# Low parts of queries and scores on VectorE, an empty step ahead of a head's first values, and one convolution product copied out of PSUM

## The chip, the cores and the metric

The kernel runs on one core of a Trainium2 chip. The metric is the device time of one execution in microseconds (us); a run's time is given as the median of several executions. The engines are named as in the profile: PE (TensorE matmuls), PEld (its weight loads), DVE (VectorE), ACT (ScalarE), POOL (GpSimd) and SP (SyncE, which issues most DMAs).

## What is computed

Two layers of a decoder trunk on 1024 tokens of width 1024. Each layer projects the normed input into eight heads of width 256 (four mLSTM heads, four retention heads), runs each head chunk by chunk, gates and norms the result, and projects it back:

```
h = rmsnorm(x) * (1 + scale) + shift;  p = h @ w_in[l]
q, k = silu(causal_dwconv(mq, mk))            # mLSTM heads; retention heads: q, k = rotary(rq, rk)
s   = einsum('bhld,bhsd->bhls', q, k) * w_intra
num = einsum('bhls,bhsv->bhlv', s, v) + w_inter * einsum('bhvk,bhlk->bhlv', C, q)
C   = decay * C + einsum('bhs,bhsv,bhsk->bhvk', w_end, v, k)
y = gated_norm(num / den);  x = x + gate * (concat(y) @ w_out[l])
```

The output is the final RMSNorm of x.

## The kernel before

**Precision.** Every float32 operand of a large product is split into a high part (a rounded copy, made by ACT) and a low part (the operand less its high part, one subtraction). A product is then three matmuls: high by high, high by low, low by high (`mm3`, L180 to L183). So each operand needs one ACT instruction and one subtraction before PE can start on it. The low parts of weights are made by `low` (L411 to L414, mostly DVE), those of queries and keys by `split_to` (L880 to L882, here always POOL), those of scores at L1084 (POOL).

**The projections.** Work on PE stands in program order. It is a list of *slots*. A slot of a q, k, z or o job is one of seven block products (a11, S1, S2, a12, S3, S4, a22) with 12 matmuls of 128x512; a slot of a value job (v) has 24 matmuls of 128x256. The products gather in PSUM banks, two of tag x and two of tag z (`ps_x`, `ps_z`). `pair_product` (L762) hands each finished piece to a `done` function. For the four mLSTM heads' q and k that is the start of `conv_chain` (L884): one ACT instruction (L889) and three DVE instructions (L894), which read the piece from where it lies. The last piece of a job, `done(1, 0, bank["X"])`, lies in PSUM, so bank X is busy until the third L894 has read it. The order of the jobs in a layer is the string `plan`.

**The attention of a head.** After each slot `tick()` runs what is due. A head's attention is the string `TABLE` (L985): one step per tick, in which `q`, `k`, `v` load a chunk's queries, keys and values, `Q` and `K` split them into high and low parts, `S` makes scores (PE L1045 and L181 to L183, then DVE L1061 to L1064 or L1073 and L1075, then ACT L1083 for the high part sH and L1084 for the low part sL), `U` updates the state, `V` makes values (PE). There are four chunks, 0 to 3. The first values of a head, `V001`, come four steps after `S0` and use no state: PE first runs the products with sH of chunk 0, then those with sL (L1126). When a head's table reaches index `RELEASE`, the next head may begin.

**The order elsewhere.** DVE, ACT, POOL and SP each work through a queue in order. That order is not written by hand: a scheduling layer sets it when the program is built, out of program order and its own estimates. Some instructions are marked to stay in program order (`late`). A small change of the program can therefore move many instructions on these engines.

**Shared buffers.** Twelve buffers of tag acc serve all intermediate 128x512 pieces; queries have two buffers, keys one, sH and sL one each.

## Time and profile before

| | |
|---|---|
| median of 3 runs | 2192.43 us (2189.73 to 2194.45) |
| the profiled execution, its own time | 2190.59 us |
| its span, first to last instruction | 2188.9 us |
| mean granted TensorE clock | 0.989 |
| PE busy | 2105.7 us (96%) |
| DVE busy | 1775.1 us (81%) |
| ACT busy | 1149.3 us (53%) |
| POOL busy | 671.1 us (31%) |

The span is what the instruction records cover; the execution's own time is 1.7 us longer. The table of waits lists, for an engine, who waited for whom: total us, times, longest. Rows of the groups by line give busy us and mean ns of one. Rows of the windows give, for each stretch of the span, the busy us of each engine with the number of instructions that began in it, then the granted clock (PEclk), the share of the DMA engines and GB/s.

### The profile page before, as it was taken

The page shows a single profiled execution, that of the slowest core. Times are in us where ns is not written, and L with a number is a line of the kernel's source. Part 1 is how long each engine was busy: PE and PEld are TensorE (multiplying, and loading weights), DVE is VectorE, ACT ScalarE, POOL GpSimd, SP SyncE. Part 2 cuts the span into 40 slices and gives each one's busy share as a digit, 9 for nine tenths or more (in the row PEclk, how much of TensorE's full clock was granted, in tenths as well). Part 3 has the DMA queues.
Part 4 walks back from the last instruction along what each step waited for, and adds up shares of the span by engine and source line. Part 5 has one row for each costly group of instructions (what it writes and reads, how often), then busy time and mean ns, then how long its engine had stood idle before and what let it go on. Part 6 is the DMA issues. An engine that isn't in the chain of part 4 may idle for free.

```text
span 2188.9 us, 34934 instructions
## 1 busy us (share of the span) xinstructions
PE 2105.7 (96%) x11489; PEld 1818.2 (83%) x11489; DVE 1775.1 (81%) x3287; ACT 1149.3 (53%) x2151; POOL 671.1 (31%) x616
## 2 busy tenths in 40 slices
PE   7899999999999999999999999999999999999998
PEld 5698889887988778888887889788988887888887
DVE  6897897999889898874639688898898888978563
ACT  7545335345565656653545434444556565665343
POOL 1421123233232333324565113322323332231313
PEclk9999999999999999999999999999999999999999
DMA  8268779788787767786633777977876676687874
GB/s 292 60 202 236 219 220 269 205 225 235 195 236 191 188 179 215 195 273 230 209 108 93 188 196 210 252 204 215 230 196 193 187 220 189 185 205 248 228 252 119
DMA packets 451971, 448.43 MB, mean 205 GB/s; under 512 B 191218, under 2 KB 308410, under 8 KB 451788
## 3 DMA queue, kind: packets, MB, share of 16 engines
q1 hardware_dynamic: 432060, 410.27, 61.3%
q0 software_dynamic: 19584, 35.66, 10.7%
q8 instruction: 90, 1.47, 0.3%
q14 instruction: 93, 0.76, 0.1%
q10 hardware_dynamic: 144, 0.26, 0.0%
HBM read 322.76 MB, written 123.31 MB: 204 GB/s over the span
## 4 chain that ended last, share of the span: by engine, by line
PE 47%; DVE 11%; DMA 5%; issue 3%; ACT 1%; POOL 1%; SPq 1%; DVEq 0%; POOLq 0%; ACTq 0%
PE px L181 6%; PE px L182 6%; PE px L183 6%; PE pz L181 5%; PE pz L182 5%; PE pz L183 4%; PE pa L183 4%; PE pa L181 3%; PE pa L182 3%; DVE R L413 2%; DVE acc L894 2%; PE pa L1135 1%; DMA acc<-kfr 1%; PE pa L1045 1%; DVE R L718 1%
## 5 line engine op out<-in xcount | busy, mean ns | idle before, releaser
L408 ACT CAST wH<-R 128x512 fp32r<-128x512 f32 x616 | 378.9, 618 | 494.4 <-PE px L182 161.0
L413 DVE TENSOR_TENSOR R<-R,wH 128x512 fp32r<-128x512 f32 x544 | 404.2, 748 | 123.4 <-ACT wH L408 121.1
L181 PE MATMUL px<-b,wH 128*128 128x512 f32 x912 | 359.9, 395 | 3.5 <-ACT acc L780 2.7
L182 PE MATMUL px<-b,wH 128*128 128x512 f32 x912 | 358.6, 393 | 0.0
L183 PE MATMUL px<-b,R 128*128 128x512 f32 x912 | 358.0, 393 | 0.0
L182 PE MATMUL pz<-b,wH 128*128 128x512 f32 x704 | 275.3, 391 | 1.6 <-DVE b L1271 1.6
L181 PE MATMUL pz<-b,wH 128*128 128x512 f32 x704 | 276.5, 393 | 0.0
L183 PE MATMUL pz<-b,R 128*128 128x512 f32 x704 | 275.0, 391 | 0.0
L714 POOL DMA_DIRECT2D R<-in_w_blk_dram x104 | 92.6, 890 | 379.1 <-DMA R<-in_w_blk_dram 191.1
L181 PEld LDWEIGHTS px<-b,wH 128*128 128x128 f32 x912 | 172.9, 190 | 39.1 <-ACT acc L780 3.9
L183 PEld LDWEIGHTS px<-b,R 128*128 128x128 f32 x912 | 172.9, 190 | 37.3
L182 PEld LDWEIGHTS px<-b,wH 128*128 128x128 f32 x912 | 172.8, 189 | 32.9
L181 PE MATMUL px<-wH,b 128*128 128x256 f32 (+1 forms) x576 | 173.2, 301 | 13.8 <-DVE acc L894 5.0
L182 PE MATMUL px<-R,b 128*128 128x256 f32 (+1 forms) x576 | 172.4, 299 | 8.3 <-DVE R L413 8.3
L183 PE MATMUL px<-wH,b 128*128 128x256 f32 (+1 forms) x576 | 171.9, 298 | 0.0
L183 PEld LDWEIGHTS pz<-b,R 128*128 128x128 f32 x704 | 132.5, 188 | 28.4
L182 PEld LDWEIGHTS pz<-b,wH 128*128 128x128 f32 x704 | 132.8, 189 | 27.5 <-DVE b L1271 2.4
L181 PEld LDWEIGHTS pz<-b,wH 128*128 128x128 f32 x704 | 132.8, 189 | 25.9 <-ACT acc L780 0.4
L882 POOL TENSOR_TENSOR kc<-acc,kc 128x512 fp32r<-128x512 f32 x64 | 91.7, 1434 | 193.3 <-ACT kc L881 169.3
L413 POOL TENSOR_TENSOR R<-R,wH 128x512 fp32r<-128x512 f32 x72 | 96.6, 1344 | 164.8 <-ACT wH L408 145.8
L882 POOL TENSOR_TENSOR q<-acc,q 128x512 fp32r<-128x512 f32 x64 | 93.5, 1461 | 131.8 <-ACT q L881 123.5
L181 PE MATMUL pz<-wH,b 128*128 128x256 f32 (+1 forms) x448 | 133.8, 299 | 0.0
(348 smaller groups left out, 5203.9 us busy)
## 6 DMA issues: line engine op xcount, KB each, us to landing
R<-in_w_blk_dram SPq DMA_DIRECT2D x276, 256.0 KB
vdr<-acc SPq DMA_DIRECT2D x128, 256.0 KB
ring<-vdr SPq DMA_DIRECT2D x64, 512.0 KB
R<-in_w_out_dram SPq DMA_DIRECT2D x128, 256.0 KB
R<-in_w_blk_dram POOLq DMA_DIRECT2D x104, 256.0 KB, 4.7
R<-in_w_val_dram SPq DMA_DIRECT2D x80, 256.0 KB
gdr<-acc SPq DMA_DIRECT2D x64, 256.0 KB
acc<-in_w_ada_dram SPq DMA_DIRECT2D x64, 256.0 KB
```

The lines of the kernel that those rows point to most:

```text
L181: PE.matmul(o, lt[0], rt[0], start=start, stop=False, skip_group_check=more)
L182: PE.matmul(o, lt[0], rt[1], start=False, stop=False, skip_group_check=more)
L183: PE.matmul(o, lt[1], rt[0], start=False, stop=stop, skip_group_check=more)
L408: A.copy(h, r)
L413: eng.tensor_tensor(lo, r, f(h), ALU.subtract)
L714: G.dma_start(raw[n], src, accum_op=ALU.add)
L718: V.tensor_tensor(raw[n], raw[one], raw[two], ALU.add)
L882: eng.tensor_tensor(dst[1], src, f(dst[0]), ALU.subtract)
L894: V.scalar_tensor_tensor(acc[:, e:], pt[:, o + e - d:o + HALF - d], wcol, acc[:, e:], ALU.mult, ALU.add)
L1045: PE.matmul(pd, piece(kx[j], i, dt, tt * P, P), qd, start=dt == 0 and i == 0, stop=dt == 1 and i == 1)
L1135: PE.matmul(pi[:, 0:W], piece(qs[j], i, dt, tt * P, P), state[part][:, dt, 0:W], start=part + dt + i == 0, stop=ml and part + dt == 2)
```

## The change

Four edits, all in the code shown above:

- The low part of a query chunk is subtracted by DVE; that of a key chunk stays on POOL (`split_qk`).
- The low part of the scores is subtracted by DVE (in `scores`).
- `TABLE` has an empty step between `Q1` and `V001 t1`, and one empty step less between `V21` and `V30`; `RELEASE` goes from 22 to 23, so it still names the step of `S3`.
- A q or k job of an mLSTM head that is followed by a value job copies its last product from bank X to an acc buffer by ACT, and its convolution reads the copy. In the two plans that is `k0` in the first layer and `k1` in the second.

```diff
-    def pair_product(F, done, loose=False, conv=False):
+    def pair_product(F, done, loose=False, conv=False, free=False):
...
                     halo("S1", bank["X"])
-                    done(1, 0, bank["X"])
+                    last = bank["X"]
+                    if free:
+                        last = wt("acc", 512, NACC)
+                        A.copy(last, bank["X"])
+                    done(1, 0, last)
...
-    TABLE = ("q0 k0 d0 t0", "", "v0", "Q0 K0 m0 d1", "s0 k1", "S0", "m1 q1 K1", "v1", "Q1", "V001 t1", "S1 k2 q2", "U01",
+    TABLE = ("q0 k0 d0 t0", "", "v0", "Q0 K0 m0 d1", "s0 k1", "S0", "m1 q1 K1", "v1", "Q1", "", "V001 t1", "S1 k2 q2", "U01",
              "s1 d2 K2", "v2 Q2", "V10 U2 m2", "S2", "t2 d3", "V11 U3 k3", "s2 q3", "v3 K3", "Q3 m3", "V20 U4",
-             "S3", "", "V21 U5", "", "", "", "V30", "V31", "")
-    RELEASE = 22
+             "S3", "", "V21 U5", "", "", "V30", "V31", "")
+    RELEASE = 23
...
-                split_to((t[:, 0:512], t[:, 512:1024]), raw)
+                split_to((t[:, 0:512], t[:, 512:1024]), raw, V if what == "q" else G)
...
-            G.tensor_tensor(lo, src, f(hi), ALU.subtract)
+            V.tensor_tensor(lo, src, f(hi), ALU.subtract)
...
-            return pair_product(F, conv_done(l, h, which), conv=True)
+            return pair_product(F, conv_done(l, h, which), conv=True, free=free)
...
-                going[j] = job_product(*jobs[j])
+                going[j] = job_product(*jobs[j], j + 1 < len(jobs) and jobs[j + 1][0] == "v")
```

In the changed kernel, lines behind L794 have numbers higher by 4 (L882 becomes L886, L1084 becomes L1088, L1126 becomes L1130).

**Low parts.** Before, on POOL, in the second mLSTM head of the first layer (kc and q are low parts of keys and queries, sL that of the scores of chunk 0, dm a mask that is read from a DMA's landing):

```order
L882 TENSOR_TENSOR kc_8696<-acc_8618,kc_8696 128x512
L714 DMA R_8737<-in_w_blk_dram 128x512
L882 TENSOR_TENSOR q_8761<-acc_8694,q_8761 128x512
L1034 AFFINE_SELECT dm_8941<-dm_8941 128x128 x2
L1084 TENSOR_TENSOR sL_8727<-acc_8646,sH_8726 128x384
L714 DMA R_8951<-in_w_blk_dram 128x512
L1185 TENSOR_TENSOR rsd_8833<-va_8832,mhalf 128x2
L882 TENSOR_TENSOR kc_8943<-acc_8852,kc_8943 128x512
```

The same two subtractions now, on DVE, among the low parts of weights (R), the convolutions (L898, L903) and a transpose of an earlier chunk (zt):

```order
L903 SCALAR_TENSOR_TENSOR acc_8606<-acc_8716,acc_8606 128x512
L413 TENSOR_TENSOR R_8783<-R_8638,wH_8762 128x512
L898 SCALAR_TENSOR_TENSOR acc_8657<-acc_8561,cols_497,acc_8657 128x512
L886 TENSOR_TENSOR q_8759<-acc_8690,q_8759 128x512
L1088 TENSOR_TENSOR sL_8727<-acc_8625,sH_8726 128x384
L1201 STREAM_TRANSPOSE zt_8755<-nd_8566 128x2x8x32
L413 TENSOR_TENSOR R_8834<-R_8467,wH_8786 128x512
L898 SCALAR_TENSOR_TENSOR acc_8657<-acc_8561,cols_497,acc_8657 128x512
```

What stood on POOL behind a load and a mask stands on DVE behind weights' and convolutions' work; the keys' subtraction is alone on POOL.

**The empty step.** Before, on PE, the end of the fourth slot behind the scores of that head's chunk 0, then its first values (ring holds the value chunk):

```order
L181 MATMUL pz_8768<-b_1256,wH_8663 128x512
L182 MATMUL pz_8768<-b_1257,wH_8663 128x512
L183 MATMUL pz_8768<-b_1256,R_8704 128x512
L1126 MATMUL pa_8786<-ring_353,sH_8726 128x258 x2
L1126 MATMUL pa_8789<-ring_353,sH_8726 128x258 x4
L1126 MATMUL pa_8786<-ring_353,sL_8727 128x258
L1126 MATMUL pa_8789<-ring_353,sL_8727 128x258 x2
```

Now a fifth slot, on the px bank, stands between the pz slot and the values; its end reads:

```order
L181 MATMUL px_8421<-b_1573,wH_8698 128x512
L182 MATMUL px_8421<-b_1574,wH_8698 128x512
L183 MATMUL px_8421<-b_1573,R_8730 128x512
L1130 MATMUL pa_8812<-ring_353,sH_8726 128x258 x2
L1130 MATMUL pa_8815<-ring_353,sH_8726 128x258 x4
L1130 MATMUL pa_8812<-ring_353,sL_8727 128x258
L1130 MATMUL pa_8815<-ring_353,sL_8727 128x258 x2
```

So 60 instead of 48 matmuls stand between scores and first values here. Where two heads overlap, the last two value steps of the earlier head (`V30`, `V31`) lay in that interval too; now only `V31` does, and the count goes from 69 to 72.

**The copy.** Before, on ACT, at the end of job `k1` of the second layer (px_19489 is the bank X of that job, acc_19799 the convolution's sum):

```order
L408 CAST wH_19943<-R_19695 128x512
L1107 CAST cH_19774<-cf_19331 128x516
L897 ACTIVATE acc_19759<-acc_19678 128x512
L889 ACTIVATE acc_19799<-px_19489,cols_1153 128x512
L889 ACTIVATE acc_19810<-acc_19538,cols_1153 128x512
```

Now, at the same place (px_19449 is that bank):

```order
L901 ACTIVATE acc_19739<-acc_19626 128x512
L1194 ACTIVATE nd_19499<-nd_19499,nmu_19741,rsd_19694 128x256
L797 COPY acc_19763<-px_19449 128x512
L1194 ACTIVATE nd_19499<-nd_19499,nmu_19741,rsd_19694 128x256
L408 CAST wH_19915<-R_19664 128x512
L893 ACTIVATE acc_19765<-acc_19763,cols_1153 128x512
L893 ACTIVATE acc_19773<-acc_19491,cols_1153 128x512
```

The copy is the last reader of the bank on ACT, and the convolution's reads (L893 and the three L898 on DVE) name the copy.

More of the change, by code (lines that the diff above doesn't have):

```diff
@@ L1623, in tile_hybrid_trunk, with job_product @@
         launch(adaptive(l, gcol, gb), 40 if l else 30)
-        def job_product(what, arg):
+        def job_product(what, arg, free=False):
             h = arg[0]
```

## The prediction

> **What bounds the kernel now.** I read the page first, then PE's waits, then the granted clock behind the longest of them, then the order of events at three places. The page's engine line, and its line of DVE's busy tenths in 40 slices of the span:

> ```profile
> PE 2105.7 (96%) x11489; PEld 1818.2 (83%) x11489; DVE 1775.1 (81%) x3287; ACT 1149.3 (53%) x2151; POOL 671.1 (31%) x616
> ...
> DVE  6897897999889898874639688898898888978563
> ```

> PE is busy 2105.7 of 2188.9 us and none of its matmuls go away, so the change can only act on the other 83 us and on PE's clock. DVE has a 9 (90% or more) in 11 of 40 slices and an 8 in 17 more: it is the next to become the bound. PE's waits, those that the edits touch and the largest that they don't:

> ```profile
> PE px L182 <- DVE R L413: 8.3, 3, 5.6
> ...
> PE pa L1126 <- ACT sH L1083: 8.2, 4, 4.1
> PE pa L1126 <- POOL sL L1084: 6.3, 7, 2.9
> ...
> PE px L181 <- DVE acc L894: 5.0, 1, 5.0
> ...
> PE pa L183 <- POOL kc L882: 3.1, 3, 1.3
> ```

> First values (L1126) cost 8.2 + 6.3 = 14.5 us, bank X behind a convolution 5.0, low parts of keys 3.1. A long stall costs a second time. Windows of 4 us at three first values and behind the convolution stall:

> ```profile
> 544.00:548.00 4.00, 2.65 (x11) 2.27 (x12) 4.00 (x6) 1.43 (x4) 2.64 (x3) 0.67 0.85 226
> 548.00:552.00 4.00, 4.00 (x10) 3.04 (x10) 1.58 (x7) 1.09 (x2) 1.48 (x3) 0.50 0.97 315
> 726.00:730.00 4.00, 4.00 (x13) 3.15 (x12) 1.18 (x9) 0.40 (x2) 1.00 (x2) 0.57 0.84 189
> 1408.00:1412.00 4.00, 3.12 (x10) 2.59 (x10) 4.00 (x10) 1.64 (x4) 2.25 (x3) 0.62 0.85 280
> 1720.00:1724.00 4.00, 3.89 (x22) 3.89 (x23) 4.00 (x11) 2.33 (x5) 2.74 (x3) 0.63 0.05 15
> ```

> PEclk is the figure after the busy times. At 0.50 a window does half its work, so the loss is 4 us times (1 - PEclk): 1.3 + 2.0 at 544, 1.7 at 726, 1.5 at 1408, which is 6.5 us behind first values, and 1.5 us behind the convolution.

> **First values: empty step and scores' low part.** At the head whose instruction order is shown above, PE and POOL:

> ```profile
> 709.36 0.40 PE L181 MATMUL pz<-b,wH 128*128 128x512 f32 x1
> ...
> 721.10 1.00 PE L1126 MATMUL pa<-ring,sH 128*128 128x258 f32 x6 [0.69 <-ACT sH L1083]
> 724.99 0.63 PE L1126 MATMUL pa<-ring,sL 128*128 128x258 f32 x3 [2.89 <-POOL sL L1084]
> ```

> ```profile
> 722.06 1.91 POOL L1034 TENSOR_SCALAR_AFFINE_SELECT dm<-dm 128x128 f32<-128x128 f32 x2 [3.51 <-DMA dm<-mdr]
> 723.95 0.98 POOL L1084 TENSOR_TENSOR sL<-acc,sH 128x384 fp32r<-128x384 f32 x1
> ```

> The 48 matmuls of four slots run from 709.36 to 720.41 (721.10 less the wait), so one takes 11.05 / 48 = 0.23 us and a slot 2.8 us. POOL was idle, but a mask that waits for its DMA stood ahead of sL. Here the fifth slot covers sH (0.69 late), and DVE can make sL without the mask: both waits go. In the heads where `V30` leaves the interval, the cover grows from 69 to 72 matmuls: twelve long ones in, nine short ones out. Six of the short kind begin within 1.00 us above, at most 0.17 apart, and half a long one's 0.23 is the least, so the gain is 12 x 0.23 less 9 x 0.12 to 0.17: 1.2 to 1.7 us, say 1.6. Of that kind is the longest stall:

> ```profile
> 543.61 0.28 DVE L1064 TENSOR_TENSOR acc<-acc 128x128 f32<-128x128 f32 x1
> ```

> ```profile
> 544.74 0.51 PE L1126 MATMUL pa<-ring,sH 128*128 128x256 f32 x2 [4.08 <-ACT sH L1083]
> ```

> What came last is the DVE queue: the scores' last DVE instruction ended at 543.9, sH a little later. If DVE comes no earlier, 4.08 - 1.6 = 2.5 us stays; the new order does put the scores' rows a little nearer to the front. Of 14.5 + 6.5 = 21 us I leave 3: **-18 us** (from -21, all gone, to -9, if the stalls that DVE ends stay with their clock).

> [...] The row at 726 shows 0.57 behind stalls of 0.69 and 2.89 us, so I keep the rows.

> **The copy.** ACT, DVE and PE around job `k1` of the second layer:

> ```profile
> 1707.70 0.76 ACT L889 ACTIVATE acc<-px,cols 128x512 f32<-128x512 f32 x1
> ```

> ```profile
> 1719.33 0.73 DVE L894 SCALAR_TENSOR_TENSOR acc<-px,cols,acc 128x509 f32<-128x509 f32 x1
> ```

> ```profile
> 1720.11 0.58 PE L181 MATMUL px<-wH,b 128*128 128x256 f32 x1 [5.04 <-DVE acc L894]
> ```

> ACT first read the bank at 1707.70; DVE's last read ended at 1720.06, and PE stood from 1715.07. A copy in L889's place ends some 7 us ahead of PE's need. Two copies of about 0.6 us on ACT (53% busy) cost nothing unless ACT comes 7 us late. Bank X's stall and clock go, 6.5 us; another DVE wait may follow, so **-6 us** (0 to -6.5). In the first layer no such wait is listed, and the copy brings nothing.

> **The load on DVE and POOL.** Forms of the instructions moved and their nearest kin (form, count, busy, mean ns):

> ```profile
> L413 DVE TENSOR_TENSOR R<-R,wH 128x512 fp32r<-128x512 f32 x544 | 404.2, 748 | 123.4 <-ACT wH L408 121.1 <-POOL b L1324 1.5
> L882 POOL TENSOR_TENSOR q<-acc,q 128x512 fp32r<-128x512 f32 x64 | 93.5, 1461 | 131.8 <-ACT q L881 123.5 <-issue 3.6 <-DMA acc<-kfr 2.6
> L882 POOL TENSOR_TENSOR kc<-acc,kc 128x512 fp32r<-128x512 f32 x64 | 91.7, 1434 | 193.3 <-ACT kc L881 169.3 <-DMA acc<-qdr 9.4 <-PE pa L183 6.6
> L1084 POOL TENSOR_TENSOR sL<-acc,sH 128x384 fp32r<-128x384 f32 x32 | 39.1, 1223 | 61.4 <-ACT sH L1083 28.3 <-DVE R L413 19.6 <-PE pa L183 13.4
> L1084 POOL TENSOR_TENSOR sL<-acc,sH 128x256 fp32r<-128x256 f32 x32 | 29.2, 912 | 95.6 <-ACT sH L1083 72.2 <-DVE cf L1104 15.1 <-issue 5.2
> ```

> POOL loses 93.5 + 39.1 + 29.2 = 161.8 us. DVE gains 64 x 0.748 = 48 us for queries and, at about 0.5 us each by their share of 512 elements and a fixed part, 32 us for 64 scores: **+80 us**. But POOL's subtractions hold DVE up now:

> ```profile
> L413 DVE TENSOR_TENSOR R<-R,wH x544: 626/682/4651, 21.5 to 2126.0; 128x512 fp32r<-128x512 f32 x182
> ```

> ```profile
> 667.38 3.74 DVE L894 SCALAR_TENSOR_TENSOR acc<-acc,cols,acc 128x512 f32<-128x512 f32 x1
> ```

> ```profile
> 668.04 1.28 POOL L882 TENSOR_TENSOR kc<-acc,kc 128x512 fp32r<-128x512 f32 x1
> 669.29 1.28 POOL L882 TENSOR_TENSOR q<-acc,q 128x512 fp32r<-128x512 f32 x1
> ```

> A DVE instruction lasted 3.74 us until POOL had done a key and a query. L413's median is 682 ns and its mean 748: 544 x 0.066 = 36 us lost in 544 of DVE's 3287 instructions. If the others with two tensors in SBUF lose alike, the whole loss is a few times 36. Queries and scores are 161.8 of POOL's 671.1 us, a quarter, and of its long subtractions more; I take 40 us of relief (0 to 161.8). Net DVE **+40 us** (+80 to -82). Whether that is time shows where DVE is full:

> ```profile
> 520.00:540.00 20.00, 20.00 (x104) 17.19 (x103) 19.68 (x37) 13.30 (x26) 6.22 (x5) 1.00 0.69 195
> 540.00:560.00 20.00, 15.31 (x68) 12.52 (x68) 14.01 (x30) 10.12 (x22) 9.05 (x9) 0.83 0.86 238
> ```

> DVE is full for 20 us (19.68), then has 6 us to spare. By the tenths, 11 slices of 40 are that full and most others nearly so; I let half of 40, 20 us, arrive as lateness, and I let half of that be caught by the lead that low parts have (two slots of 2.8 us or more between a Q step and its S step). With 2 us of clock behind new stalls: **+12 us** (0 to +45, the latter with no relief and as much clock again).

> The moved instructions also wait, and behind them on DVE stand low parts of weights, for which PE waits. ACT's high part of queries is late itself:

> ```profile
> ACT q L881 <- DMA acc<-qdr: 39.3, 23, 3.5
> ```

> Most of that lies ahead of DVE's arrival, since DVE runs later than ACT in the full stretches; I put it inside the 12.

> **Keys.** With no query ahead on POOL, the 3.1 us should fall: **-2 us** (0 to -3.1).

> **Sum.** -18 - 6 - 2 + 12 = -14 us against the profiled execution's own 2190.6: 2176.6. The median lies 1.8 us above that execution, so 2178 us; with the terms' middle parts, 2170 to 2186.

> **Rivals.** *All is gained* (18%): relief covers the load, as L1034's mask and the 3.74 us suggest: -21 - 6.5 - 3.1 gives 2162 us (2158 to 2170). *The empty step does little* (7%): stalls that end with DVE stay, -9 for first values: 2187 us. *Given back* (14%): DVE, 20 us behind in full stretches, makes PE wait at the next weight's low part or bank for what it no longer waits at first values: 2188 to 2197 us. *Slower* (15%): a query's subtraction on DVE and a key's on POOL now start in the same step and hold each other up. From the point where both high parts are ready together, DVE is second and stands for the key's 1.43 us, 64 times, 92 us. With the net 40 that is 132; a quarter by the rule above, 33, and 5 of clock, less the 26 gained: +12, or 2204 us (2197 to 2215). For it speaks the 3.74 us; against it L413's mean, only 0.066 us over its median though POOL works beside it.

> [...]

> **Chances.** The forecast's own case has 46%. A measurement here can tell about 0.2%, 4.4 us. Faster by more: 46 + 18 + 6 of the 7 = 70%; within: 1 + 14 = 15%; slower: 15%. The range leaves out the outer third of the best case and most of the slow one: 2162 to 2198 us.

> **What would show it.** In the changed profile: L1130's waits under 4 us in all and no half clock behind them; no wait of PE for L898 near 1715; POOL near 510 us and DVE near 1815; L413 with the same count and a mean nearer to 682 ns. The forecast is wrong if PE's waits for R L413 or for queries' low parts (L886) grow past 15 us, or if DVE's busy time ends above 1840.

## The result, and the profile after

The changed kernel is slower: 2201.5 us (2197.1 to 2206.0, 7 runs) against 2190.4 us for the kernel before on the same chip, a ratio of 1.0046 with a 95% interval of 1.0034 to 1.0058, or some 10 us. The forecast was 2178 us. All comparisons below are with runs of the kernel before on the same chip, and leave disturbed runs out.

The engine line and VectorE's busy tenths of the changed kernel:

```profile
PE 2110.7 (96%) x11489; PEld 1824.9 (83%) x11489; DVE 1780.7 (81%) x3415; ACT 1151.7 (52%) x2153; POOL 514.6 (23%) x488
...
DVE  6897897999889899875549697898898888978563
```

POOL is down by 156.5 us, as forecast, but DVE is up by only 5.6, not by 40. The span is 2200.2 us, 11.3 more: PE is busy 5.0 us longer and, by the gaps between its matmuls, idle 81.5 instead of 75.2 us up to its last one. PE's waits, those that matter:

```profile
PE pa L183 <- DVE sL L1088: 16.0, 8, 3.4
PE pa L183 <- DVE b L938: 12.9, 9, 3.0
...
PE px L182 <- DVE R L413: 7.9, 2, 5.6
...
PE px L181 <- ACT acc L834: 3.4, 1, 3.4
...
PE pa L182 <- DVE q L886: 1.3, 2, 0.7
...
PE pa L1130 <- DVE sL L1088: 1.0, 1, 1.0
...
PE pa L183 <- POOL kc L886: 0.8, 1, 0.8
```

At first values (L1130) 1.0 us is left of 14.5. In their place stand two waits further on in a head, at L183: for sL of the later chunks, 16.0 us where the whole list of before has 0.6, and for the low part of the transposed keys (b, L938, `k_split`), 12.9 where before has 5.4 (L934). All three are made by DVE.

The first of these waits, seen from the engines at one place:

```profile
747.40 0.39 ACT L1087 CAST sH<-acc 128x256 fp32r<-128x256 f32 x1
...
747.98 0.65 DVE L413 TENSOR_TENSOR R<-R,wH 128x512 fp32r<-128x512 f32 x1
...
748.55 0.69 DVE L787 TENSOR_TENSOR acc<-px,acc 128x512 f32<-128x512 f32 x1
...
749.15 0.74 DVE L898 SCALAR_TENSOR_TENSOR acc<-acc,cols,acc 128x512 f32<-128x512 f32 x1
...
749.80 0.75 DVE L898 SCALAR_TENSOR_TENSOR acc<-pz,cols,acc 128x509 f32<-128x509 f32 x1
...
750.46 0.88 DVE L938 SCALAR_TENSOR_TENSOR b<-acc,wd,b 128x256 fp32r<-128x256 f32 x2
...
751.25 0.43 DVE L1088 TENSOR_TENSOR sL<-acc,sH 128x256 fp32r<-128x256 f32 x1
...
751.73 0.58 PE L183 MATMUL pa<-ring,sL 128*128 128x258 f32 x1 [3.38 <-DVE sL L1088]
```

sH is there at 747.79. Before DVE comes to sL at 751.25 it makes a weight's low part, an addition, two taps of a convolution (L898) and two low parts of keys, without a pause, and PE stands for 3.38 us. How full DVE is at such places, and what the clock does, in windows of 4 us at six of these stalls:

```profile
750.00:754.00 4.00, 2.27 (x9) 2.18 (x10) 4.00 (x8) 1.73 (x3) 0.96 (x2) 0.50 1.01 275
...
1434.00:1438.00 4.00, 2.96 (x11) 2.47 (x12) 4.00 (x8) 0.99 (x2) 0.68 (x1) 0.74 0.42 80
1520.00:1524.00 4.00, 3.17 (x16) 3.17 (x17) 3.85 (x9) 2.07 (x5) 0.72 (x2) 0.65 0.87 323
1888.00:1892.00 4.00, 3.55 (x15) 2.99 (x16) 4.00 (x10) 1.25 (x2) 0.00 (x0) 0.73 0.80 164
1828.00:1832.00 4.00, 3.95 (x11) 3.14 (x12) 4.00 (x10) 1.17 (x3) 1.16 (x1) 0.57 0.00 0
1916.00:1920.00 4.00, 3.09 (x10) 2.63 (x11) 4.00 (x12) 1.09 (x2) 0.88 (x1) 0.65 0.61 229
```

The third busy figure is DVE's: 4.00 of 4 us in five of them, 3.85 in the sixth. The figure after the five busy times is PEclk: each stall has a stretch at half clock within it or right behind it. In the clock record these stretches are 3.41 us long or a multiple of it; 12 such lengths lie before PE's end in the kernel before, 18 in the changed one, and each costs PE up to 1.7 us, about half of what it would do in it: there a 128x512 matmul begins 0.43 us behind the one before it, at full clock 0.23 us (medians, the same in both kernels).

### The profile page after: what moved, and what is told of

The parts are those of the page before. It is cut to its first block, busy times and chain, and to the rows that moved or that the text cites. A ratio compares the mean times of both kernels' runs of the same rounds, so it can differ in the third digit from the quotient of the medians.

```text
span 2200.2 us, 34892 instructions
## 1 busy us (share of the span) xinstructions
PE 2110.7 (96%) x11489; PEld 1824.9 (83%) x11489; DVE 1780.7 (81%) x3415; ACT 1151.7 (52%) x2153; POOL 514.6 (23%) x488
## 4 chain that ended last, share of the span: by engine, by line
PE 63%; DVE 19%; DMA 9%; issue 5%; ACT 2%; SPq 1%; POOL 0%; DVEq 0%; POOLq 0%; ACTq 0%
PE px L181 9%; PE px L182 8%; PE px L183 8%; PE pz L181 7%; PE pz L182 7%; PE pz L183 6%; PE pa L183 4%; PE pa L181 4%; PE pa L182 4%; DVE R L413 3%; DVE acc L898 2%; PE pa L1139 2%; DMA R<-in_w_blk_dram 1%; DMA acc<-qdr 1%; PE pa L1049 1%
## 5 line engine op out<-in xcount | busy, mean ns | idle before, releaser
L408 ACT CAST wH<-R 128x512 fp32r<-128x512 f32 x616 | 379.0, 619 | 520.3 <-PE px L182 159.8
L413 DVE TENSOR_TENSOR R<-R,wH 128x512 fp32r<-128x512 f32 x544 | 388.5, 719 | 92.2 <-ACT wH L408 89.3
L181 PE MATMUL px<-b,wH 128*128 128x512 f32 x912 | 357.9, 392 | 0.8 <-ACT acc L780 0.8
L182 PE MATMUL px<-b,wH 128*128 128x512 f32 x912 | 356.7, 391 | 0.0
L183 PE MATMUL px<-b,R 128*128 128x512 f32 x912 | 356.6, 391 | 0.0
L182 PE MATMUL pz<-b,wH 128*128 128x512 f32 x704 | 277.0, 393 | 2.9 <-DVE b L1275 2.9
L181 PE MATMUL pz<-b,wH 128*128 128x512 f32 x704 | 278.0, 395 | 0.0
L183 PE MATMUL pz<-b,R 128*128 128x512 f32 x704 | 276.6, 393 | 0.0
L183 PEld LDWEIGHTS px<-b,R 128*128 128x128 f32 x912 | 171.8, 188 | 36.8
L181 PEld LDWEIGHTS px<-b,wH 128*128 128x128 f32 x912 | 172.1, 189 | 35.1 <-ACT acc L780 1.7
L182 PEld LDWEIGHTS px<-b,wH 128*128 128x128 f32 x912 | 172.1, 189 | 33.1
L181 PE MATMUL px<-wH,b 128*128 128x256 f32 (+1 forms) x576 | 174.8, 304 | 10.4 <-DVE acc L968 3.6
L182 PE MATMUL px<-R,b 128*128 128x256 f32 (+1 forms) x576 | 174.1, 302 | 7.9 <-DVE R L413 7.9
L183 PE MATMUL px<-wH,b 128*128 128x256 f32 (+1 forms) x576 | 173.8, 302 | 0.0
L886 POOL TENSOR_TENSOR kc<-acc,kc 128x512 fp32r<-128x512 f32 x64 | 92.9, 1451 | 320.0 <-ACT kc L885 289.1
L182 PEld LDWEIGHTS pz<-b,wH 128*128 128x128 f32 x704 | 133.8, 190 | 29.4 <-DVE b L1275 3.7
L183 PEld LDWEIGHTS pz<-b,R 128*128 128x128 f32 x704 | 133.6, 190 | 28.7
L181 PEld LDWEIGHTS pz<-b,wH 128*128 128x128 f32 x704 | 134.0, 190 | 26.2 <-issue 0.2
L1189 POOL TENSOR_TENSOR rsd<-va,mhalf 128x2 f32<-128x2 f32 x64 | 60.3, 942 | 339.8 <-DVE va L1182 174.2
L181 PE MATMUL pz<-wH,b 128*128 128x256 f32 (+1 forms) x448 | 134.6, 301 | 0.7 <-DVE acc L790 0.7
L182 PE MATMUL pz<-R,b 128*128 128x256 f32 (+1 forms) x448 | 134.3, 300 | 0.0
```

What stands on the lines that cost most here:

```text
L181: PE.matmul(o, lt[0], rt[0], start=start, stop=False, skip_group_check=more)
L182: PE.matmul(o, lt[0], rt[1], start=False, stop=False, skip_group_check=more)
L183: PE.matmul(o, lt[1], rt[0], start=False, stop=stop, skip_group_check=more)
L408: A.copy(h, r)
L413: eng.tensor_tensor(lo, r, f(h), ALU.subtract)
L886: eng.tensor_tensor(dst[1], src, f(dst[0]), ALU.subtract)
```

## The experiments

Theories at the start: **S** and **Q**, the low parts of scores or of queries on DVE cost the time; **N**, the kernel before is a tuned point of the order and any move costs. Behind e3 came **A**: the empty step moves everything behind the first values by a slot into DVE's convolution work. When A fell (e9, e10), **B** took its place: where DVE is full it sets PE's pace, and a wait that is taken away at the first values comes back at the next operand that DVE makes.

### e1 to e3: low parts back on POOL

The `V` of the scores' subtraction made `G` again in the changed kernel (e1), that of the queries' (e2), and both (e3, empty step and copy alone).

```diff
-            V.tensor_tensor(lo, src, f(hi), ALU.subtract)
+            G.tensor_tensor(lo, src, f(hi), ALU.subtract)
```

> The changed kernel with the scores' low part back on POOL; queries' low part on DVE, empty step and copy stay. Theory S (in the DVE queue the scores' low part of chunks 1 to 3 comes too late; that is PE's 16.0 us on sL L1088 in the changed profile and the clock behind it): PE's waits for sL outside the first values fall from 16 to under 3 us, half-clock stretches from 17 to about 12, time about 2180 us, ahead of the kernel before by 10. Theory Q (queries' low part on DVE delays everything else there, k's low part L938 above all): L938 stays near 12.9 us, time 2193 to 2200. Theory N (any new order of the queues costs or gains some 10 us at random): a time that fits neither, with new waits in places that the edit doesn't touch.

> The changed kernel with the queries' low part back on POOL; scores' low part on DVE, empty step and copy stay. Theory S: the waits for sL stay near 16 us and the time near 2200. Theory Q: the waits for k's low part (L938) fall from 12.9 to about the 5.4 us of before, those for sL to half since DVE has 44 us less to do, time about 2185. Theory N: waits move about, time anywhere from 2185 to 2210.

> The changed kernel with both low parts back on POOL: only the empty step and the copy are left. Theories S and Q: first values no longer wait (L1130 under 3 us against 14.5 before), no sL wait in chunk 1 beyond 1 us, time about 2178 (12 less than before: 14.5 of waits and about 6 us of clock, less the half that other waits take up). Theory N: within 5 us of before, with as much waiting in other places.

Measured: e1 2202.4 us (1.0060 [1.0041, 1.0079]), e2 2198.2 us (1.0044 [1.0028, 1.0061]), e3 2213.7 us (1.0116 [1.0096, 1.0136]). Neither subtraction taken back alone gains anything that can be told from noise, and both taken back lose some 14 us more (e3 is 25.4 us above before on its chip, the changed kernel 11.1). S and Q fall, and with them the forecast's rival that a query on DVE and a key on POOL hold each other up: beside the empty step the low parts on DVE save time. In e1 PE waits 14.5 us for sL of later chunks although POOL makes it, so it is not the engine of the subtraction alone that is late.

### e4 to e6: the edits apart

e4 is the changed kernel without the copy, e5 the kernel before with the new `TABLE` and `RELEASE` alone, e6 the changed kernel with the old ones.

```diff
-                going[j] = job_product(*jobs[j], j + 1 < len(jobs) and jobs[j + 1][0] == "v")
+                going[j] = job_product(*jobs[j])
```

```diff
-    TABLE = ("q0 k0 d0 t0", "", "v0", "Q0 K0 m0 d1", "s0 k1", "S0", "m1 q1 K1", "v1", "Q1", "V001 t1", "S1 k2 q2", "U01",
+    TABLE = ("q0 k0 d0 t0", "", "v0", "Q0 K0 m0 d1", "s0 k1", "S0", "m1 q1 K1", "v1", "Q1", "", "V001 t1", "S1 k2 q2", "U01",
...
-             "S3", "", "V21 U5", "", "", "", "V30", "V31", "")
-    RELEASE = 22
+             "S3", "", "V21 U5", "", "", "V30", "V31", "")
+    RELEASE = 23
```

> The changed kernel without the copy of a convolution's last product. If the copy gains what its stall cost (5.0 us and 1.7 us of clock, less the 3.4 us that PE now waits for ACT's copy of the value job just behind it), this one is 2 to 4 us slower than the changed kernel: 2204. If the stall is only passed on to the next wait, it is the same within 2 us. Theory N: off by 5 us or more either way.

> The kernel before with the empty step alone (the new table and RELEASE 23); both low parts on POOL, no copy. With the copy beside it this stood at 2213.7 us. Theory A (the step sets all of a head from its first values on one slot later against the projections, so that scores of chunk 1 and the keys' low part L938 come into DVE's convolution work; the step is the loss, the low parts on DVE are a gain): 2208 to 2215 us, first values under 4 us, PE's waits for sL of chunk 1 about 9 and for L938 about 11 us. Theory N (the order of the queues is new with every edit, and that alone is worth 10 to 25 us): a time between 2185 and 2205, as the copy's removal makes another order.

> The changed kernel with the old table and RELEASE 22: low parts of queries and scores on DVE and the copy, no empty step. Theory A: faster than before. Of the 14.5 us of first values those that POOL ended (6.3) go, the convolution's 5.0 goes, the waits for sL in chunk 1 and for L938 are as before (under 1 and about 5 us): 2178 to 2184 us. Theory S (the low parts on DVE lose): 2195 or above. Theory N: anything from 2180 to 2205.

Measured: e4 2199.3 us (1.0050 [1.0034, 1.0066]), e5 2210.1 us (1.0094 [1.0076, 1.0111]), e6 2196.8 us (1.0032 [1.0020, 1.0044]). The copy is worth nothing here. The step alone, with no work moved between engines, costs 21 us. Its waits:

```profile
PE pa L183 <- POOL sL L1084: 14.4, 8, 3.9
PE pa L183 <- DVE b L934: 12.8, 10, 2.1
PE px L182 <- DVE R L413: 8.3, 3, 5.6
...
PE px L181 <- DVE acc L964: 6.4, 2, 3.9
PE px L181 <- ACT acc L780: 6.3, 3, 2.9
PE px L181 <- DVE acc L894: 4.5, 1, 4.5
```

The two waits of the changed kernel are here as well, without its low parts: the step alone brings them. sL has POOL's name, but POOL waits for sH, and sH for the scores' last instruction on DVE: measured from the scores' end, DVE finishes those of chunk 1 after 8.7 us on average instead of 6.8 in the kernel before. But e6, for which A expected a gain, loses some 7 us without the step, at L938 (14.9 us) and behind a bank (ACT acc L834, 9.7 us), so not all of the loss, and not every wait for L938, is the step's.

### e7 and e8: the head moved against the projections

e7 is the kernel before with heads launched one slot later (a delay of 5 ticks instead of 4). e8 is the changed kernel with the empty step taken from the head's start, so that the scores come one slot earlier and the first values stay where they were before the change. In e8 some loads stand ahead of the stores whose data they read, so it computes something else.

```diff
-                launch(attention(l, jobs[j][1][0], gt), 4, 1)
+                launch(attention(l, jobs[j][1][0], gt), 5, 1)
```

```diff
-    TABLE = ("q0 k0 d0 t0", "", "v0", "Q0 K0 m0 d1", "s0 k1", "S0", "m1 q1 K1", "v1", "Q1", "", "V001 t1", "S1 k2 q2", "U01",
+    TABLE = ("q0 k0 d0 t0", "v0", "Q0 K0 m0 d1", "s0 k1", "S0", "m1 q1 K1", "v1", "Q1", "", "V001 t1", "S1 k2 q2", "U01",
...
-             "S3", "", "V21 U5", "", "", "V30", "V31", "")
-    RELEASE = 23
+             "S3", "", "V21 U5", "", "", "", "V30", "V31", "")
+    RELEASE = 22
```

> The kernel before with every head launched five slots behind its key job instead of four; table, RELEASE and engines as before, so a head that waits for the head ahead of it is not moved. Theory A: the same shift of chunk 1 and the keys against the projections as by the empty step, with no more cover for first values: sL waits of chunk 1 of 5 us or more and L938 of 8 or more, time 2200 to 2210 us. Against A: waits for sL in chunk 1 stay under 2 us and the time within 4 us of before.

> The changed kernel, but the empty step ahead of the first values is paid for by the empty step between a head's first and second loads (index 1), and RELEASE is 22: scores of chunk 0 come one slot earlier, first values and all behind them stand at the slots of the kernel before. Theory A: first values wait under 2 us, sL of chunk 1 and L938 as before (under 2 and about 5 us), the convolution's stall gone, 2168 to 2178 us; the price is keys' and queries' high parts on ACT that may come too late for the scores (up to 5 us more). Theory S or N: 2195 or above, with sL waits as in the changed kernel.

Measured: e7 2212.4 us (1.0103 [1.0086, 1.0120]), with 19.6 us of waits for L934, while its first values still wait 13.6 us (9.7 for sL, 3.9 for sH); e8 2211.4 us (1.0102 [1.0085, 1.0118]), where the waits for sL are gone, but PE waits 11.6 us for value chunks from DMA, 10.4 for ACT's high part of keys and 10.0 for a bank behind ACT. e8 shows no more than that the scores can be moved out of that wait at the price of others, since its own edit puts its loads out of order.

### e9 and e10: the first values alone, one slot later

V001 goes into the step of S1 (with t1, a load of keys), so it comes one slot later, and every other step stays where it was before the change: in the changed kernel (e9) and in the kernel before (e10, shown).

```diff
-    TABLE = ("q0 k0 d0 t0", "", "v0", "Q0 K0 m0 d1", "s0 k1", "S0", "m1 q1 K1", "v1", "Q1", "V001 t1", "S1 k2 q2", "U01",
+    TABLE = ("q0 k0 d0 t0", "", "v0", "Q0 K0 m0 d1", "s0 k1", "S0", "m1 q1 K1", "v1", "Q1", "", "V001 t1 S1 k2 q2", "U01",
```

> The changed kernel, with the first values V001 put into the step of S1 (still one slot later than before) and every later step and RELEASE where they stood before the change. Theory A (the loss is that everything behind the first values moves by a slot into other work of VectorE): the first values stay covered, the waits for sL of chunk 1 fall under 4 us and the time comes to 2172 to 2188 us, faster than before. Theory N (the kernel before is a tuned point of the scheduler's order and any move of PE work costs 7 to 25 us): 2196 to 2212 us, with waits for low parts and banks at new places.

> The kernel before, with V001 put one slot later into the step of S1, and nothing else changed. Theory A: the 14.5 us of waits at first values and some of their 6.5 us of clock go, no new waits above 5 us: 2174 to 2187 us. Theory N: 2196 to 2212 us. If it is slower than e9 by more than 5 us, the low parts on VectorE help as they did beside the empty step (12 us).

Measured: e9 2205.5 us (1.0079 [1.0065, 1.0093]), e10 2208.5 us (1.0094 [1.0073, 1.0114]). A falls: nothing behind the first values was moved, and the loss is as large as with the whole step. The waits of e10:

```profile
PE pa L183 <- DVE b L934: 13.6, 10, 3.4
...
PE pa L181 <- ACT b L933: 8.1, 5, 3.3
PE px L181 <- ACT acc L780: 7.5, 5, 4.1
PE px L181 <- DVE acc L894: 5.9, 2, 5.0
PE px L181 <- DVE acc L964: 4.9, 2, 2.5
```

At first values (L1126) 3.0 us is left of 14.5, 1.8 for sL and 1.2 for sH. PE waits instead for keys' parts, for banks, and for a chain of convolutions, on DVE and ACT. Where the time goes is seen by comparing the same projection matmul in each kernel. The columns: its start in the kernel before (us), and how much later it starts in the others, at places between heads where nothing is shifted by a slot; worked out from the traces:

```
before   after     e5    e10     e6    e12
   283    +0.6   -0.2   -0.4   +0.6   -0.4
   396    +4.9   +2.2   +4.2   +1.9   +1.0
   896    -0.5   +5.7   +5.7   +4.9   -1.3
  1274    +0.1   +6.0   +5.8   +3.0   -1.2
  1552    +1.7  +11.0  +13.8   -0.8   -2.7
  1765    +2.8  +16.1  +17.7   +2.8   -1.6
  1976   +11.0  +20.7  +23.3   +8.3   -3.2
```

The gains of the first values are in these numbers already. The changed kernel is level with before at 1274 and loses 8 us in the last overlap of heads, between 1765 and 1976; e6, without the step, loses 5.5 us there.

At one head the gain and its loss can be followed, between matmuls that no slot shifts: e10 is 6.7 us later than before at 720, only 1.0 at 740, behind the first values, and 8.6 at 760. In the kernel before DVE is busy 5.00 of the 5 us from 715, 3.73 of those from 720, where PE stands, and 1.36 of those from 725: it catches up. In e10 it is busy 5.00, 5.00, 4.75 and 4.91 us in the four stretches of 5 us from 720 on. PE then waits 1.3 us for L933 and 3.4 for L934 (before: 1.1 in all), with a clock of 0.50 from 750 to 755 (before: 1.00). A full DVE is not the whole story even there, for ahead of that work it stood 1.50 us itself, for POOL (L1185).

### e11 and e12: a small disturbance, and the copy on the kernel before

e11 swaps two loads in a head's first step. PE's order is unchanged by it, and on DVE only neighbours change places. e12 is the kernel before with the copy alone (the edit of L794 as in the change).

```diff
-    TABLE = ("q0 k0 d0 t0", "", "v0", "Q0 K0 m0 d1", "s0 k1", "S0", "m1 q1 K1", "v1", "Q1", "V001 t1", "S1 k2 q2", "U01",
+    TABLE = ("k0 q0 d0 t0", "", "v0", "Q0 K0 m0 d1", "s0 k1", "S0", "m1 q1 K1", "v1", "Q1", "V001 t1", "S1 k2 q2", "U01",
```

> The kernel before with the loads of the keys ahead of those of the queries in a head's first step: PE's order is the same, and VectorE's differs at a hundred or so rows that change places with neighbours. It gauges what any small disturbance of the order costs. Theory A: 2186 to 2194 us, no change. Theory N: slower by 7 us or more, 2197 us or above.

> The kernel before with the copy alone. As forecast (the bank's stall and its clock go): 2182 to 2186 us. Passed on (another wait of an equal size follows behind it, as the ScalarE wait of 3.4 us did in the changed kernel): 2187 to 2192 us. Theory N: 2196 us or above.

Measured: e11 2196.6 us (2188.8 to 2202.7, 11 runs; 1.0032 [1.0014, 1.0051]); its profiled run took 2189.9 us and shows no wait that explains the median. e12 2189.9 us (1.0012 [0.9997, 1.0028]). So a nearly neutral edit can cost up to 7 us, which is as much as e6 lost: that loss can't be put down to its edits. N holds for sizes of that kind, but not yet for 20 us.

### e15 and e16: the waited-for step one slot earlier

The steps s1 and s2 of the keys' low parts, on the changed kernel (e15) and on before (e16).

```diff
-    TABLE = ("q0 k0 d0 t0", "", "v0", "Q0 K0 m0 d1", "s0 k1", "S0", "m1 q1 K1", "v1", "Q1", "", "V001 t1", "S1 k2 q2", "U01",
-             "s1 d2 K2", "v2 Q2", "V10 U2 m2", "S2", "t2 d3", "V11 U3 k3", "s2 q3", "v3 K3", "Q3 m3", "V20 U4",
+    TABLE = ("q0 k0 d0 t0", "", "v0", "Q0 K0 m0 d1", "s0 k1", "S0", "m1 q1 K1", "v1", "Q1", "", "V001 t1", "S1 k2 q2", "U01 s1",
+             "d2 K2", "v2 Q2", "V10 U2 m2", "S2", "t2 d3", "V11 U3 k3 s2", "q3", "v3 K3", "Q3 m3", "V20 U4",
```

> The changed kernel with the steps s1 and s2 (low parts of keys for the state update, L938, on VectorE) one slot earlier, in the steps of U01 and V11. If the waits for L938 (12.9 us) and their half-clock windows are a matter of which slot of convolution work the step falls into, they fall under 5 us and the time comes to 2186 to 2195 us. Theory B: VectorE has the same work to do, the wait moves to sL, R or a bank, 2197 to 2205 us. Theory N: 2200 to 2215 us.

> The kernel before with the same two steps one slot earlier: the control for e15. A matter of slots: L934's 5.4 us of waits fall to about 2, 2184 to 2190 us. Theory B: 2186 to 2192 us, no change. Theory N: 2195 us or above.

Measured: e15 2199.9 us (1.0056 [1.0043, 1.0069]), e16 2187.4 us (0.9994 [0.9982, 1.0007]). The waits of e15:

```profile
PE pa L183 <- DVE sL L1088: 17.7, 9, 2.7
...
PE px L181 <- ACT acc L834: 7.0, 3, 4.3
PE pa L182 <- DVE q L886: 6.8, 3, 3.4
...
PE pa L181 <- ACT sH L1087: 4.4, 4, 2.4
```

Not one wait for L938 is left of 12.9 us, and the time is what it was (in e16 the 5.4 us for L934 are gone as well, at no gain): sL has 1.7 us more, queries' low parts 5.5, L834 3.6, sH 0.8, together 11.6. The wait went to the next operand, as B says.

### e13, e14, e17 and e18: the same edits where DVE has less to do

Two of the four convolution taps are left out, which are 128 of DVE's instructions, all in the slots of the convolutions. e13 is the kernel before so lightened, e14 the changed kernel, e17 before with the step alone (as e5), e18 the changed kernel without the step (as e6).

```diff
-        for d in range(1, 4):
+        for d in range(1, 2):
```

> The kernel before with one instead of three multiply-adds of VectorE in each convolution piece (two of the four taps are left out of the computation): some 100 us less of VectorE's 1775, all of it in the slots where it is full. It is the reference for e14. Theory B (where VectorE is full it sets PE's pace, and a wait taken away at the first values comes back at its next low part): waits for low parts of keys (L934) and for banks behind the convolution fall, 2170 to 2184 us, while the 14.5 us at first values stay at 8 or more. Theory N (the order before is a tuned point, whatever VectorE's load): slower than before, 2192 us or above, since this too changes the order.

> The changed kernel with the same two taps left out. Theory B: with VectorE no longer full the gain at first values is kept, and it is 8 to 20 us faster than e13 (about 2155 to 2172 us). Theory N: it stays 5 to 15 us slower than e13, as the changed kernel is against before.

> The kernel before with the empty step alone (as e5) and with the two taps left out (as e13). In e5 the step cost 21 us against the kernel before. Theory B (a full VectorE turns the gain at first values into later waits): without that fullness the cost is gone, 2150 to 2163 us, against 2160.7 for e13. Theory N: 2172 us or above, 12 or more above e13.

> The changed kernel without the empty step (as e6) and with the two taps left out. In e6 these edits cost 7 us. Theory B: they cost 0 to 3 us, 2158 to 2164 us. If the 7.5 us between e13 and e14 come from the lows and the copy and not from the step, it is at 2150 to 2156 us and e17 at 2160 or above.

Times against the kernel before, and against their own counterpart:

| edits | all taps, us | ratio to before | one tap, us | ratio to before |
|---|---|---|---|---|
| none | 2189 to 2190 | 1 | e13 2160.7 | 0.9876 [0.9864, 0.9889] |
| step alone | e5 2210.1 | 1.0094 [1.0076, 1.0111] | e17 2154.5 | 0.9838 [0.9821, 0.9854] |
| all but the step | e6 2196.8 | 1.0032 [1.0020, 1.0044] | e18 2149.4 | 0.9814 [0.9798, 0.9829] |
| all | after 2201.5 | 1.0046 [1.0034, 1.0058] | e14 2153.2 | 0.9835 [0.9822, 0.9847] |

The sign turns in each case. With all taps the edits cost 7 to 21 us; with one tap they gain 6.2 (step), 11.3 (the rest) and 7.5 us (all), with intervals that don't touch e13's. e13 keeps the waits at first values:

```profile
PE pa L1126 <- POOL sL L1084: 8.1, 9, 2.5
...
PE pa L1126 <- ACT sH L1083: 3.7, 3, 2.1
```

In e14 they are gone and little has come for them:

```profile
PE pa L183 <- DVE sL L1088: 6.0, 4, 2.6
...
PE pa L183 <- DVE b L938: 3.3, 3, 1.6
...
PE pa L1130 <- DVE sL L1088: 1.4, 1, 1.4
```

PE's idle time is 57.5 us in e13 and 51.2 in e14, and the lengths of half clock go from 12 to 9. B is borne out in sign for each edit, not in every size: e13 is 9 us below its range, e14 gains a little less than the 8 us expected, and e18, which was to lose 0 to 3 us, gains. N, as a price of 10 to 20 us on any move, is not, since here the same moves gain. A weaker N is not excluded, that only the order of the kernel before with all its taps is a tuned point: leaving out taps makes a new order too, and no run changes DVE's load with the order held. The engine lines of e13 and e14 show how little it takes:

```profile
PE 2098.2 (97%) x11489; PEld 1815.5 (84%) x11489; DVE 1702.5 (79%) x3159; ACT 1145.4 (53%) x2151; POOL 666.9 (31%) x616
```

```profile
PE 2091.6 (97%) x11489; PEld 1813.7 (84%) x11489; DVE 1696.6 (79%) x3287; ACT 1148.5 (53%) x2153; POOL 506.9 (24%) x488
```

DVE is busy 79% instead of 81% of the span. The mean tells little; the 73 us less are taken from the convolutions' slots, and e13 is 29 us faster than before.

No version with all of the computation was found that beats the kernel before by more than the measurement can tell; e16 comes nearest, at 0.9994.

## Why the prediction was wrong, point by point

**First values, -18: the step that failed.** The waits went as it said: 14.5 us to 1.0 (L1130), and the half clock at 545, 726 and 1409 with them. What failed is the sentence "both waits go" taken as time. It counted this wait as a term of its own, and let lateness of DVE come only from work that the change adds. But the wait was a pause in which a full DVE caught up (in the kernel before it was busy 3.73 of the 5 us from 720 and 1.36 of those from 725). With it gone PE reaches the next operand from DVE earlier than DVE does, and stalls there: the step alone costs 21 us with DVE full (e5), 20 when nothing but V001 and t1 moves (e10), and gains 6 with DVE lighter (e17). The prediction had the row that says so, 20.00 us of PE and 19.68 of DVE in 520 to 540, just ahead of the longest first-value stall, and used it for the moved subtractions only.

**The load, +12.** Its size was off the other way: DVE's own time rose by 5.6 us, not 40. The forms of the moved instructions and of their neighbours:

```profile
L413 DVE TENSOR_TENSOR R<-R,wH 128x512 fp32r<-128x512 f32 x544 | 388.5, 719 | 92.2 <-ACT wH L408 89.3 <-POOL b L1328 1.5 <-DMA R<-in_w_blk_dram 0.3
L886 POOL TENSOR_TENSOR kc<-acc,kc 128x512 fp32r<-128x512 f32 x64 | 92.9, 1451 | 320.0 <-ACT kc L885 289.1 <-PE pa L182 11.1 <-DMA ndr<-zt 7.5
L898 DVE SCALAR_TENSOR_TENSOR acc<-acc,cols,acc 128x512 f32<-128x512 f32 x96 | 72.7, 758 | 0.0
L886 DVE TENSOR_TENSOR q<-acc,q 128x512 fp32r<-128x512 f32 x64 | 51.1, 799 | 28.3 <-ACT q L885 28.2
...
L1088 DVE TENSOR_TENSOR sL<-acc,sH 128x384 fp32r<-128x384 f32 x32 | 17.9, 560 | 0.3 <-ACT sH L1087 0.2
L1088 DVE TENSOR_TENSOR sL<-acc,sH 128x256 fp32r<-128x256 f32 x32 | 17.1, 535 | 3.9 <-ACT sH L1087 3.8
```

DVE took over 51.1 + 17.9 + 17.1 = 86.1 us, as forecast (80), and the rest of its work got 80.5 us shorter, twice the 40 allowed: L413's mean went from 748 to 719 ns, which is 15.7 us, that of these L898 from 823 to 758. The signs named for this term came out on the good side (R 7.9 us, queries 1.3, POOL 515, DVE below 1815), and the kernel was slower all the same: they watched the moved subtractions, not what PE would next wait for. Beside the step the low parts save some 14 us (e3 against after).

**The copy, -6.** No wait for L898 near 1715, as said. But from 1723.15 PE stands for 3.4 us at the next bank:

```profile
1724.58 0.75 DVE L898 SCALAR_TENSOR_TENSOR acc<-acc,cols,acc 128x512 f32<-128x512 f32 x1
...
1725.90 0.57 ACT L834 COPY acc<-px 128x512 f32<-128x512 f32 x1
...
1726.52 0.58 PE L181 MATMUL px<-wH,b 128*128 128x256 f32 x1 [3.37 <-ACT acc L834]
```

DVE is still in the convolutions there, and the half clock comes too. The text had "another DVE wait may follow" as the far end, 0; it should have been the middle (e12: 1.1 us slower than before, within its error; e4: nothing).

**Keys, -2.** 3.1 to 0.8 us, as forecast, of no use in the sum for the same reason.

**The rivals.** *Given back* (14%) had the mechanism and named the next low part or bank; its 2188 to 2197 us was too low because it let PE give back only what it had gained, with no more of half clock. *Slower* (15%) had the time, 2197 to 2215, but not the mechanism: a query's subtraction takes DVE 799 ns and not 1.43 us more than its own time, a key's on POOL is at 1451 ns where it was at 1434, and with the queries back on POOL e2 is no faster than the changed kernel by more than can be told (1.0044 against 1.0046).

**What stays open.** That B makes the gain nothing follows from the waits. Why the step then costs 21 us, and not 0, is shown in parts only: in e5 the span is 20.8 us longer, of which PE is busy 8.6 us longer, with 20 lengths of half clock where before has 12, and idle 12.3 us longer. The clock is paid anew for many of the smaller stalls. The added idle time sits in waits at single places which a full DVE makes likely and the scheduler's new order decides. Which rows of that order they hang on was not settled, nor why e11 takes 0.3% more.

## What to carry to other kernels

A stall of the bounding engine in front of a nearly full one is not a term that can be taken out of a sum (here 13.5 of 14.5 us of waits went, and the time rose by some 10): ask first what the full engine does during the stall, and which of its outputs is wanted next. Read the second engine's load in windows of some 4 us at the stalls and not as a share of the span, and test the idea by taking work off that engine: if the edit's sign turns, that speaks for the engine as the limit. The measured order of worth here is to lighten DVE in the convolution slots first (29 us for 73, here by leaving computation out), and only then to remove waits (6 to 11 us).

## What the runs showed of the hardware

Short stalls can cost as much clock as long ones. The stall of 2.10 us at 1828.05 has PEclk 0.57 in the window behind it (1828 to 1832, above), one length of half clock:

```profile
1828.05 0.39 PE L183 MATMUL pa<-ring,sL 128*128 128x258 f32 x1 [2.10 <-DVE sL L1088]
```

Moving 128 of POOL's subtractions with two inputs to DVE (168.4 us of POOL's time in e3) shortened DVE's busy time. The two kernels whose text differs in nothing else are e3, with both subtractions on POOL, and the changed kernel, whose engine line stands above; e3's is:

```profile
PE 2116.1 (96%) x11489; PEld 1828.3 (83%) x11489; DVE 1790.6 (81%) x3287; ACT 1148.6 (52%) x2153; POOL 673.0 (30%) x616
```

DVE has 128 instructions more and is busy 1780.7 instead of 1790.6 us, though the instructions moved take it 86.1 us. So, if the scheduler's new order is not the reason, the subtractions on POOL had cost DVE about 96 us, more than making them itself; the forecast, which leaned on the mean and median of L413 alone, allowed 40.
